# Where the branch for an expert's overflow tokens stands: behind the last expert pass, or in front of it

## Chip, cores and metric

One core of a Trainium2 chip runs the kernel. The metric is the device time of one execution in microseconds (us).

## What is computed

The kernel computes three transformer layers for 256 tokens of width 1024 in float32. The first layer is a block with two kinds of attention and a dense feed-forward. The second and third (here layer 0 and layer 1, as the kernel's code counts them) each have attention, a mixture of 32 experts in four groups, and a gated projection of a per-layer embedding. The expert part and the part behind it, cut from the reference:

```python
def hier_moe(xn, w_group, b_group, w_expert, b_expert, w_gate, w_up, w_down):
    ...
    e_w, e_idx = lax.top_k(e_prob, TOPK_IN_GROUP)          # 2 of the 8 experts of one group
    ...
    cw = jnp.einsum('tk,tke->te', comb, jax.nn.one_hot(expert_id, N_EXPERTS, ...))
    hid = jax.nn.silu(jnp.einsum('td,edf->tef', xt, w_gate)) * jnp.einsum('td,edf->tef', xt, w_up)
    y = jnp.einsum('tef,efd->td', hid * cw[:, :, None], w_down)
    return y.reshape(b, s, d)

# in second_block, for each layer i, behind the attention:
h = h + hier_moe(rms_norm_2(h, ln_ffn[i]), ...)
gate = jax.nn.sigmoid(rms_norm_2(h, ln_ple[i]) @ ple_w_gate[i])
h = h + (gate * (p[i] @ ple_w_proj[i])).astype(h.dtype)
```

## The kernel before

**The expert part** is `moe(l, router, rs)`. It goes over the 32 experts in eight passes `q` of four. Each expert has 32 places for tokens, so a pass has 128 rows. `pick` (in `steps`) builds `T.d`, a 0/1 matrix of tokens by places, on VectorE. A pass then consists of

- `gather` (L993): PE multiplies the activations `hr` with `T.d`, which gives `T.xe`, the tokens in their places;
- `slots` (L1009, L1011): PE transposes `T.d` and fetches the weights of the tokens; ScalarE writes the transposed matrix back into `T.d`;
- `gate_up` (L1025): 64 matmuls of the four experts' gate and up weights against `T.xe`, then `hidden` (L1032 on ScalarE, L1033 and L1034 on VectorE);
- `turn` (L1038 a transpose on PE, L1039 its copy on ScalarE) and `down` (L1045, 16 matmuls; L1049 and L1050 write the result as two parts, `yd`);
- `combine` (L1056): eight matmuls that add `yd` back to the tokens in the four PSUM accumulators `acc`, which also hold the residual.

In the loop, `combine` of pass q - 1 is issued behind `gate_up(q)`, so that PE has work while `hidden(q)` runs on the other engines. For the last combine, L1061 copies the accumulators to `h`.

**Overflow.** If an expert has more than 32 tokens, the rest goes through `Overflow`. `find` picks an expert, `load` fetches its weights (from pass 4 on), and `run` does all of the above for one expert with up to 128 places: `gather` (L993), the transposes L1120 and L1122, 16 matmuls L1129, `turn`, four matmuls L1134, and `combine`. How many such jobs there are is only known on the chip. `over.all` therefore issues the steps in a runtime branch on the count `njob`: `tc.If(n > 0)` around one `run` (L1142), and in it `tc.If(n > 1)` with a loop (L1144, L1145). All five engines take part in the branch, SyncE too. With these inputs layer 0 has one job and layer 1 none.

**Weights** come as a stream: `W.next` hands out pieces of an arena (tiles named `a`), and SyncE issues the loads in the stream's order, each as soon as its piece is free. Behind the experts' weights stand `ple_g` (the gate of the embedding, four loads), then `b_w_q`, the shared key/value weights and `b_w_out` of the next attention. `W.room` and `drop` decide when pieces are free. Tiles of activations (`take`) live in the same arena.

**Behind the experts** comes `ple(l, ...)`: `xt_feats` transposes `h` on PE (L503) and writes it as two parts (`a` at L520 on ScalarE, L521 on VectorE); `proj` multiplies it with `ple_g`, whose tiles are split into two parts (L538, L539), in three matmuls per product (L543 to L545); `gated_part` starts with a tanh at L1226. Eight k steps of six matmuls make one half of the columns; in both layers they are the first thing that runs.

Of the kernel before, what the change touches and what calls it, by code (L numbers as in the profile page):

```python
# [251 lines left out]
def block_kernel(ctx, tc, I, out):  # L252
# [14 lines left out]
    def bank(name="bank"):  # L267
        return psum.tile([128, 512], F32, tag="bank", name=name)

    def sq2(name="sq"):  # L270
        return pr.tile([128, 512], F32, tag="sq", name=name)
# [12 lines left out]
    def drop(*keys):  # L284
        for k in keys:
            arena.drop(k)
        W.pump()
# [120 lines left out]
    def C(name, rows=128):  # L408
        o, n = _COLS[name]
        return cst[:rows, o:o + n]  # L410
# [14 lines left out]
    def drain(g):  # L425
        for _ in g:
            pass
# [22 lines left out]
    def rest(n):  # L450
        for _ in range(n):
            yield

    def chain(*gens):
        for g in gens:
            yield from g
# [26 lines left out]
    class Rstd:  # L483
        def __init__(self, name):
            self.ss = tiny.tile([128, 2, 2], F32, tag="ss", name="ss")
            self.name = name
# [314 lines left out]
    def ple_load(l):  # L801
        pv_ = sq2("ple_p").rearrange("p (t n) -> p t n", t=2)
        nc.sync.dma_start(pv_, I["p_2"][l, 0].rearrange("(t p) n -> p t n", p=128))
        return pv_
# [10 lines left out]
    def ple_proj(pT):  # L815
        pj = take("pj", [2, 1024])
        name, ws = W.next("ple_p")
        for c in range(2):
            ps = [bank("pj") for _ in range(2)]
            for k in range(2):  # L820
                acc_k(pT, k, ws[k][:, c * 512:(c + 1) * 512], ps, k == 0, k == 1)
                yield
            for t in range(2):
                A.copy(pj[:, t, c * 512:(c + 1) * 512], ps[t])
        W.drop(name)
        drop("pT")
        pjs.append(pj)
# [3 lines left out]
    class Step:  # L831


        def __init__(self, d, beside=None):
            self.ahead = ahead = beside is not None
            if ahead:
                self.banks = [bank("ov") for _ in range(3)]
            self.d, self.gub = d, None
            self.sq = beside.sq[:, 256:512] if ahead else sq2("hd")
            self.th, self.hd = self.sq[:, 0:128], self.sq[:, 128:256]  # L840
            self.hT = self.th
            self.ej = tiny.tile([128, 2, 4], F32, tag="ej", name="ej", bufs=4)
            self.cs = tiny.tile([128, 2], F32, tag="cs", name="cs", bufs=4)
            self.xe = self.xet() if ahead else None
            self.yd = [self.ydt() for _ in range(2)] if ahead else []

        def xet(self):
            return sring.tile([128, 8, 128], F32, tag="s", name="xe")
# [14 lines left out]
    def new_d(n):  # L863
        return pr.tile([128, 2, n], F32R, tag="sq", name="d")

    def moe(l, router, rs):
# [114 lines left out]
        def gather(d, Ts, banks=None):  # L981
            Ts = list(Ts)
            n = 128 * len(Ts)
            m = 512 // n
            for T in Ts:
                if not T.ahead:
                    T.xe = T.xet()
            for j in range(8 // m):
                b = bank("g") if banks is None else banks[j % 2]
                for t in range(2):  # L990
                    for i in range(m):
                        for hl in range(2):
                            mm(b[:, i * n:(i + 1) * n], hr[hl][:, t, (m * j + i) * 128:(m * j + i) * 128 + 128], d[:, t],  # L993
                               start=t + i + hl == 0, stop=t + i + hl == m + 1)
                bv = b.rearrange("p (k e s) -> p k e s", k=m, e=len(Ts))
                for e, T in enumerate(Ts):
                    mv = m // 2 if len(Ts) == 1 else m if e == 0 else 0
                    ks = slice(m * j, m * j + mv)
                    if mv:
                        V.tensor_tensor(T.xe[:, ks], bv[:, 0:mv, e],  # L1000
                                        gp[:, ks].unsqueeze(2).to_broadcast([128, mv, 128]), OP.mult)
                    for i in range(mv, m):
                        A.activation(T.xe[:, m * j + i], bv[:, i, e], AF.Copy, scale=gp[:, m * j + i:m * j + i + 1])
                yield

        def slots(q, T):
            b = T.bank("ex")
            for t in range(2):
                nc.tensor.transpose(b[:, t * 128:(t + 1) * 128], T.d[:, t].bitcast(F32), ident)  # L1009
            for t in range(2):  # L1010
                mm(b[:, 256:266], T.d[:, t], cwr[:, t, q], start=t == 0, stop=t == 1)  # L1011
            yield
            A.copy(T.d, b[:, 0:256].rearrange("p (t n) -> p t n", t=2))
            parts = b[:, 256:266].rearrange("p (a e) -> p a e", a=2)
            V.tensor_tensor_reduce(out=T.ej, in0=parts[:, :, 0:4], in1=C("emask").unsqueeze(1).to_broadcast([128, 2, 4]),
                                   scale=1.0, scalar=0.0, op0=OP.mult, op1=OP.add, accum_out=T.cs[:, 0:1])
            V.tensor_reduce(T.cs[:, 1:2], parts[:, :, 4], AX.X, OP.add)
# [34 lines left out]
        def combine(T, last):  # L1052
            for c in range(2):
                for hl in range(2):
                    for t in range(2):
                        mm(acc[t][c], T.d[:, t], T.yd[c][:, hl],  # L1056
                           start=False, stop=last and hl == 1)
                if last:
                    with tc.high_priority():
                        for t in range(2):  # L1060
                            (A.copy if t else V.tensor_copy)(h[:, t, c * 512:(c + 1) * 512], acc[t][c])  # L1061

        class Overflow:
# [75 lines left out]
            def all(self, T, n):  # L1139
                R = Step(new_d(128), T)  # L1140
                self.pick(R.d)
                with tc.If(n > 0):  # L1142
                    self.run(R)
                    with tc.If(n > 1):  # L1144
                        with tc.For_i(1, n, 1):  # L1145
                            self.find()
                            self.load()
                            self.pick(R.d)
                            self.run(R)
                drop("ovg", "ovd", "ovf")  # L1150

        nrs = Rstd(f"rp{l}")
        prev = None
        for q in range(8):
            names, gu, dn = [], [], []
            if q == 6:
                combine(prev, False)
                prev = None
                drain(ple_proj(ple_T(pv_)))
            for i in range(6):  # L1160
                name, v = W.next("gate_up" if i < 4 else "down")
                names.append(name)
                (gu if i < 4 else dn).append(v)
            if q == 2:
                pv_ = ple_load(l)
            if q == 2:
                W.room(4)
            if q == 3:
                over = Overflow()
            if q == 4:  # L1170
                over.load()
                njob_r = nc.values_load(njob_i[0:1, 0:1], min_val=0, max_val=32)
            if q == 5:
                W.room(6 if l else 9)
            if q == 0:
                g = gather(d, Ts)
                next(g)
                acc_h(1, 1)
            T = Ts.pop(0)
            ahead = not Ts and q < 7  # L1180
            if ahead:
                d, Ts = steps()
            if q == 0:
                for i, _ in enumerate(gate_up(0, T, gu)):
                    if i == 1:
                        drain(g)
                        drain(slots(0, T))
                    W.drop(names.pop(0))
            else:
                drain(gate_up(q, T, gu))  # L1190
            if prev is not None:
                combine(prev, False)
            while len(names) > 2:
                W.drop(names.pop(0))
            fill = chain(gather(d, Ts) if ahead else (), slots(q + 1, Ts[0]) if Ts else ())
            for _ in range(0 if q else 3):
                next(fill, None)
            turn(T)
            for _ in range(9 if q else 1):
                next(fill, None)  # L1200
            down(T, dn)
            drain(fill)
            for name in names:
                W.drop(name)
            prev = T
        over.all(T, njob_r)
        drop("hr0", "hr1")
        h = take("h", [2, D])
        combine(T, True)

# [873 lines left out]
```

## Time and profile before

| | before |
|---|---|
| median of 3 runs | 864.68 us (860.13 to 865.07) |
| the profiled execution | 864.54 us |
| its span | 862.8 us |
| PE busy | 823.1 us, 95% of the span |
| DVE, ACT, POOL busy | 61%, 52%, 26% of the span |
| moved by DMA | 201.71 MB, mean 234 GB/s |
| mean granted PE clock | 0.988 of full speed |

[...] The span runs from the first to the last instruction of the trace; what the execution takes beyond it lies outside. Times in rows are microseconds from the span's start. In the page's second part the span is cut into 40 slices of 21.57 us. An "idle before" names what ended it: "DMA" a transfer, an engine's name with "q" its sequencer, "issue" nothing that the profile shows. Consecutive matmuls overlap, so the step from one row to the next is the time of a row, rather than its own duration.

### The profile page before, as it was taken

Reading aid. Unit: us, or ns where it says so; the run is one execution under the profiler, and the core shown is the slowest. Engines: PE = TensorE matmul, PEld = TensorE weight load, DVE = VectorE, ACT = ScalarE, POOL = GpSimd, SP = SyncE. Lnnn points to the kernel's source line nnn. Section 1 sums busy time; section 2 is a strip of 40 time slices with the busy share of each in tenths; the row PEclk is TensorE's granted clock in tenths of the full one; section 3 lists DMA queues with packets and bytes.
Section 4 is the critical chain, followed back from the end, with each engine's and each line's share of the span. In section 5 each row is a group of like instructions: output and inputs, shape, how many; then the busy total and the mean of one; then the engine's idle time right before and its main releaser. Section 6 shows DMA issues by size and latency. Waiting matters only on the chain. (4 is left out here: it accounts for less than half of the span.)

```text
span 862.8 us, 15686 instructions
## 1 busy us (share of the span) xinstructions
PE 823.1 (95%) x5660; PEld 642.2 (74%) x5660; DVE 522.4 (61%) x1520; ACT 447.0 (52%) x1085; POOL 224.3 (26%) x293
## 2 busy tenths in 40 slices
PE   8998999999999999999899999986999999999787
PEld 6896878999999988686667666645878677667456
DVE  5778766755454567678874635423688757353355
ACT  5676865544444456367774133423677743333353
POOL 1224542322222233314553200000224434000011
PEclk9999999999999999999999999999899899999999
DMA  9991529655555542455015699999853426899961
GB/s 320 385 373 43 178 78 398 227 194 167 192 182 194 195 156 99 130 176 208 37 55 198 252 381 404 408 403 377 305 182 124 183 91 258 297 403 406 409 236 49
DMA packets 85714, 201.71 MB, mean 234 GB/s; under 512 B 5840, under 2 KB 27776, under 8 KB 85632
## 3 DMA queue, kind: packets, MB, share of 16 engines
q1 hardware_dynamic: 83568, 198.36, 63.2%
q10 hardware_dynamic: 2064, 2.29, 0.9%
q8 instruction: 47, 0.77, 0.4%
q14 instruction: 35, 0.29, 0.1%
HBM read 199.57 MB, written 1.06 MB: 233 GB/s over the span
## 5 line engine op out<-in xcount | busy, mean ns | idle before, releaser
L539 DVE TENSOR_TENSOR s<-a,s 128x512 fp32r<-128x512 f32 (+3 forms) x281 | 189.9, 686 | 122.7 <-ACT s L538 88.5
L538 ACT CAST s<-a 128x512 fp32r<-128x512 f32 (+3 forms) x294 | 172.5, 601 | 165.6 <-PE pj L545 72.0
L543 PE MATMUL pj<-s,a 128*128 128x512 f32 (+3 forms) x456 | 177.3, 389 | 6.9 <-ACT a L520 5.4
L544 PE MATMUL pj<-s,a 128*128 128x512 f32 (+3 forms) x456 | 171.5, 376 | 3.9 <-DVE s L539 3.8
L539 POOL TENSOR_TENSOR s<-a,s 128x512 fp32r<-128x512 f32 (+3 forms) x71 | 89.3, 1258 | 313.0 <-ACT s L538 280.5
L545 PE MATMUL pj<-s,a 128*128 128x512 f32 (+3 forms) x456 | 170.6, 374 | 0.1
L543 PEld LDWEIGHTS pj<-s,a 128*128 128x128 f32 x456 | 86.8, 190 | 25.6 <-issue 6.2
L544 PEld LDWEIGHTS pj<-s,a 128*128 128x128 f32 x456 | 87.2, 191 | 18.7 <-DVE s L539 6.0
L545 PEld LDWEIGHTS pj<-s,a 128*128 128x128 f32 x456 | 86.9, 191 | 15.9 <-DVE a L521 1.1
L536 POOL TENSOR_SCALAR s<-a 128x512 fp32r<-128x512 f32 (+3 forms) x58 | 40.7, 701 | 221.7 <-PE pj L545 115.2
L1556 PE MATMUL f<-a,s 128*128 128x256 f32 x256 | 72.6, 284 | 0.0
L1558 PE MATMUL f<-a,s 128*128 128x256 f32 x256 | 72.4, 283 | 0.0
L1557 PE MATMUL f<-a,s 128*128 128x256 f32 x256 | 72.4, 283 | 0.0
L1025 PE MATMUL gu<-a,xe 128*32 128x256 f32 x1024 | 61.0, 380 | 5.0 <-DMA a<-in_moe_w_up_dram 4.3
L1025 PEld LDWEIGHTS gu<-a,xe 128*32 128x32 f32 x1024 | 33.6, 110 | 33.8 <-issue 11.5
L543 PE MATMUL acc<-s,a 128*128 128x512 f32 x128 | 50.1, 391 | 0.0
L544 PE MATMUL acc<-s,a 128*128 128x512 f32 x128 | 49.9, 390 | 0.0
L545 PE MATMUL acc<-s,a 128*128 128x512 f32 x128 | 49.8, 389 | 0.0
L1557 PEld LDWEIGHTS f<-a,s 128*128 128x128 f32 x256 | 49.1, 192 | 0.2
L1556 PEld LDWEIGHTS f<-a,s 128*128 128x128 f32 x256 | 49.1, 192 | 0.2
L1558 PEld LDWEIGHTS f<-a,s 128*128 128x128 f32 x256 | 49.1, 192 | 0.0
L640 POOL TENSOR_SCALAR P<-P,nd 128x128 f32<-128x128 f32 x64 | 30.5, 489 | 51.5 <-DVE nd L635 22.1
(359 smaller groups left out, 1413.3 us busy)
## 6 DMA issues: line engine op xcount, KB each, us to landing
a<-in_moe_w_gate_dram SPq DMA_DIRECT2D x66, 512.0 KB, 7.1
a<-in_moe_w_up_dram SPq DMA_DIRECT2D x66, 512.0 KB, 8.3
a<-in_w_ff_dram SPq DMA_DIRECT2D x32, 1024.0 KB, 5.6
a<-in_moe_w_down_dram SPq DMA_DIRECT2D x32, 1024.0 KB, 10.2
a<-in_a_w_in_dram SPq DMA_DIRECT2D x10, 1024.0 KB, 5.1
a<-in_ple_w_gate_dram SPq DMA_DIRECT2D x8, 1024.0 KB, 15.6
a<-in_w_in_dram SPq DMA_DIRECT2D x6, 1024.0 KB, 14.0
a<-in_w_o_dram SPq DMA_DIRECT2D x4, 1024.0 KB, 13.3
```

The source lines that it names most:

```text
L536: G.tensor_scalar(hi, wv, 1.0, 0.0, OP.mult, OP.add)
L538: A.copy(hi, wv)
L539: (G if nsplit[0] % 5 == 2 else V).tensor_tensor(lo, wv, hi.bitcast(F32), OP.subtract)
L543: mm(ps, xh, hi, start=st, stop=False)
L544: mm(ps, xh, lo, start=False, stop=False)
L545: mm(ps, xl, hi, start=False, stop=sp)
L640: G.tensor_scalar(p[:, o0:o0 + n], p[:, o0:o0 + n], rc[:, t, i:i + 1], 1.0, OP.mult, OP.mult)
L1025: mm(b[32 * e:32 * e + 32, 0:256], T.xe[:, k, 32 * e:32 * e + 32], w, start=k == 0, stop=k == 7)
L1556: mm(o, hi[:, fs], xt[0][:, k], start=st, stop=False)
L1557: mm(o, hi[:, fs], xt[1][:, k], start=False, stop=False)
L1558: mm(o, lo[:, fs], xt[0][:, k], start=False, stop=sp)
```

## The change

`over.all` is called in the loop at the end of pass 6 instead of behind the loop, in both layers. Three things go with it. `combine(6)`, which was issued behind `gate_up(7)`, is issued in `all`, ahead of the branch; `prev = None` keeps it from being issued again. The tiles `R.yd` of the overflow step are allocated there instead of in `Step`. And at q == 6 the filler work (`slots(7)`) goes behind `down(6)` instead of around it. The activations `hr0`, `hr1` are dropped after pass 6. Line numbers of the changed kernel are those of before plus 2 from L1142 on (the branch is L1144, its inner ones L1146 and L1147) and plus 9 behind the loop.

```diff
@@ Step.__init__
-            self.yd = [self.ydt() for _ in range(2)] if ahead else []
+            self.yd = []
@@ Overflow.all
                 self.pick(R.d)
+                combine(T, False)
+                R.yd = [R.ydt() for _ in range(2)]
                 with tc.If(n > 0):
@@ the loop over q
             fill = chain(gather(d, Ts) if ahead else (), slots(q + 1, Ts[0]) if Ts else ())
+            later = rest(0)
+            if q == 6:
+                fill, later = later, fill
             for _ in range(0 if q else 3):
                 next(fill, None)
             turn(T)
@@
             down(T, dn)
             drain(fill)
+            drain(later)
             for name in names:
                 W.drop(name)
             prev = T
-        over.all(T, njob_r)
-        drop("hr0", "hr1")
+            if q == 6:
+
+                over.all(T, njob_r)
+                drop("hr0", "hr1")
+                prev = None
         h = take("h", [2, D])
         combine(T, True)
```

PE in layer 0, the way into the branch. In the kernel before, from the combine of pass 6, which stands behind the 32 last matmuls of gate_up(7) (`y_6295`, `y_6303` are the results of down(7)):

```order
L1056 MATMUL acc<-yd,d 128x512 x8
L1038 MATMUL ht<-ident_r,hd 128x128
L1045 MATMUL y_6295<-a_6100,hd 32x512 x2
L1045 MATMUL y_6295<-a_6163,hd 32x512 x2
L1045 MATMUL y_6303<-a_6100,hd 32x512 x2
L1045 MATMUL y_6303<-a_6163,hd 32x512 x2
L1142 COMPARE_AND_BRANCH
L993 MATMUL ov<-d,a_5050 128x128
```

In the changed kernel, from the turn of pass 6 (`y_6212`, `y_6220` are the results of down(6)):

```order
L1038 MATMUL ht<-ident_r,hd 128x128
L1045 MATMUL y_6212<-a_5880,hd 32x512 x2
L1045 MATMUL y_6212<-a_5882,hd 32x512 x2
L1045 MATMUL y_6220<-a_5880,hd 32x512 x2
L1045 MATMUL y_6220<-a_5882,hd 32x512 x2
L1009 MATMUL ex<-ident_r,d 128x128 x2
L1011 MATMUL ex<-cwr,d 128x10 x2
L1056 MATMUL acc<-yd,d 128x512 x8
L1144 COMPARE_AND_BRANCH
L993 MATMUL ov<-d,a_5050 128x128
```

The branch has come forward past gate_up(7), the turn and down(7); combine(6) now stands directly in front of it, and slots(7) has moved behind down(6).

PE in layer 0, the way out of the branch, from the last matmuls of the loop's body (which is not entered) on. Before:

```order
L1056 MATMUL acc<-yd,d 128x512 x8
L1145 REGISTER_ALU
L1145 COMPARE_AND_BRANCH
L1145 UNCONDITIONAL_BRANCH
L1144 UNCONDITIONAL_BRANCH
L1142 UNCONDITIONAL_BRANCH
L1056 MATMUL acc<-yd,d 128x512 x8
L503 MATMUL tps<-ident_r,a_6524 128x128 x8
```

In the changed kernel, first the way out, and then (behind the gate_up(7) that begins there) from the turn of pass 7 on:

```order
L1056 MATMUL acc<-yd,d 128x512 x8
L1147 REGISTER_ALU
L1147 COMPARE_AND_BRANCH
L1147 UNCONDITIONAL_BRANCH
L1146 UNCONDITIONAL_BRANCH
L1144 UNCONDITIONAL_BRANCH
L1025 MATMUL gu<-a_5884,xe 32x256
```

```order
L1038 MATMUL ht<-ident_r,hd 128x128
L1045 MATMUL y_6504<-a_6100,hd 32x512 x2
L1045 MATMUL y_6504<-a_6163,hd 32x512 x2
L1045 MATMUL y_6512<-a_6100,hd 32x512 x2
L1045 MATMUL y_6512<-a_6163,hd 32x512 x2
L1056 MATMUL acc<-yd,d 128x512 x8
L503 MATMUL tps<-ident_r,a_6524 128x128 x8
```

Behind the branch now stands gate_up(7) with no combine between it and its turn, and the last combine follows down(7) with no branch between.

SyncE in layer 0, the loads in front of the branch, from the last of `ple_g` on. Before:

```order
L299 DMA a_6207<-in_ple_w_gate_dram 128x4x512
L299 DMA a_6236<-in_b_w_q_dram 128x4x512
L299 DMA a_6238<-in_b_w_q_dram 128x4x512
L299 DMA a_6284<-in_b_w_q_dram 128x4x512
L299 DMA a_6286<-in_b_w_q_dram 128x4x512
L299 DMA a_6288<-in_w_kv_shared_dram 128x8x256
L299 DMA a_6290<-in_w_kv_shared_dram 128x8x256
L299 DMA a_6311<-in_b_w_out_dram 128x4x512
L299 DMA a_6313<-in_b_w_out_dram 128x4x512
L1142 COMPARE_AND_BRANCH
```

In the changed kernel:

```order
L299 DMA a_6205<-in_ple_w_gate_dram 128x4x512
L299 DMA a_6207<-in_ple_w_gate_dram 128x4x512
L299 DMA a_6236<-in_b_w_q_dram 128x4x512
L299 DMA a_6238<-in_b_w_q_dram 128x4x512
L1144 COMPARE_AND_BRANCH
```

Six loads (two of `b_w_q`, the two shared ones and two of `b_w_out`) have moved from in front of the branch to behind it.

## Rows read from the trace of the kernel before

**Rows 1.** the page: busy time of the engines; granted clock and memory traffic in 40 slices

```profile
PE 823.1 (95%) x5660; PEld 642.2 (74%) x5660; DVE 522.4 (61%) x1520; ACT 447.0 (52%) x1085; POOL 224.3 (26%) x293
...
PEclk9999999999999999999999999999899899999999
...
GB/s 320 385 373 43 178 78 398 227 194 167 192 182 194 195 156 99 130 176 208 37 55 198 252 381 404 408 403 377 305 182 124 183 91 258 297 403 406 409 236 49
```

**Rows 2.** timeline of PE, layer 0 (start, us, engine, line, operation, count, [idle before, releaser])

```profile
568.14 0.30 PE L1038 MATMUL ht<-ident_r,hd 128*128 128x128 f32 x1 [1.37 <-DVE hd L1034]
568.28 0.38 PE L1009 MATMUL ex<-ident_r,d 128*128 128x128 f32 x2
...
568.80 1.92 PE L1045 MATMUL y<-a,hd 128*32 128x512 f32 x16
570.54 1.07 PE L1025 MATMUL gu<-a,xe 128*32 128x256 f32 x6
573.57 3.61 PE L1025 MATMUL gu<-a,xe 128*32 128x256 f32 x58 [1.96 <-DMA a<-in_moe_w_up_dram]
577.11 2.13 PE L1056 MATMUL acc<-yd,d 128*128 128x512 f32 x8
579.08 0.27 PE L1038 MATMUL ht<-ident_r,hd 128*128 128x128 f32 x1
579.71 1.92 PE L1045 MATMUL y<-a,hd 128*32 128x512 f32 x16 [0.35 <-ACT hd L1039]
581.56 3.79 PE L993 MATMUL ov<-d,a 128*128 128x128 f32 x32
...
595.80 2.11 PE L1056 MATMUL acc<-yd,d 128*128 128x512 f32 x8 [0.42 <-PEq L1144]
598.93 1.09 PE L503 MATMUL tps<-ident_r,a 128*128 128x128 f32 x8 [1.02 <-DVE a L1061]
603.65 0.80 PE L543 MATMUL pj<-s,a 128*128 128x512 f32 x1 [3.63 <-ACT a L520]
```

**Rows 3.** timeline of ACT, layer 0, the first feature write

```profile
603.13 0.47 ACT L520 ACTIVATE a<-tps,small 128x256 fp32r<-128x256 f32 x1 [3.02 <-SPq L1144]
```

**Rows 4.** timeline of SP, layer 0, the weight loads behind ple_g

```profile
577.85 10.23 SPq L299 DMA_DIRECT2D a<-in_b_w_q_dram  x4
...
596.82 8.26 SPq L299 DMA_DIRECT2D a<-in_b_w_out_dram  x4
```

**Rows 5.** timeline of PE, layer 1, passes 6 and 7 and what follows

```profile
813.77 1.92 PE L1045 MATMUL y<-a,hd 128*32 128x512 f32 x16
...
819.04 3.61 PE L1025 MATMUL gu<-a,xe 128*32 128x256 f32 x58 [1.96 <-DMA a<-in_moe_w_up_dram]
...
825.18 1.92 PE L1045 MATMUL y<-a,hd 128*32 128x512 f32 x16 [0.35 <-ACT hd L1039]
827.28 1.64 PE L1056 MATMUL acc<-yd,d 128*128 128x512 f32 x6 [0.18 <-PEq L1142]
831.41 1.01 PE L1056 MATMUL acc<-yd,d 128*128 128x512 f32 x2 [2.49 <-issue]
832.22 1.91 PE L503 MATMUL tps<-ident_r,a 128*128 128x128 f32 x8
833.84 0.80 PE L543 MATMUL pj<-s,a 128*128 128x512 f32 x1
```

**Rows 6.** DMA of the stretch 828.5 to 831 (queue, packets, MB, share)

```profile
q8 instruction: 1, 0.02, 2.8%
```

**Rows 7.** busy time by stretch; behind the engines: granted clock, DMA share, GB/s

```profile
560.00:580.00 20.00, 16.30 (x177) 9.65 (x179) 4.21 (x14) 4.99 (x11) 0.00 (x0) 1.00 1.03 405
...
602.40:609.20 6.80, 5.55 (x15) 4.48 (x16) 3.77 (x13) 5.13 (x14) 0.00 (x0) 0.50 1.07 373
...
831.10:834.50 3.40, 3.09 (x12) 2.58 (x12) 2.11 (x4) 1.39 (x3) 0.00 (x0) 0.50 0.51 187
```

**Rows 8.** line 1226, its waits for the projection, first in each layer (first, last start)

```profile
L1226 ACTq EVENT_SEMAPHORE  x2: 17/17/17, 617.0 to 844.3; - x2
```

## The prediction, made before the changed kernel was run

> **What bounds the kernel now.** The page comes first: TensorE is busy for 95% of the span and its granted clock is below full in only a few of the 40 slices [rows 1], so time is won where TensorE stands still or runs at half clock. Then the timeline of TensorE around the overflow branch, in both expert layers. In layer 0 one job exists and the body runs; three spots of that row list matter [rows 2]. Pass 7's gate/up matmuls stop for 1.96 us for the last up weight and go on at 573.57. Pass 7's own turn, down and combine follow, the body runs from 581.56, and the last combine starts at 595.80. And the first gate projection of the next stage (L543) starts only at 603.65, after 3.63 us of idle. What ends last there is ScalarE: its first L520, the write of the transposed features, sat 3.02 us for "SPq L1144" [rows 3]. It writes into the arena piece that held the overflow weights, so it needs SyncE to have passed the branch, and SyncE has queued six more weight loads in front of that branch: its issues run from 577.85 to 605.1 [rows 4], over 2 us each, while memory moves 377 to 408 GB/s [rows 1]. In layer 1 no job exists and the branch is jumped [rows 5]: the last combine begins at 827.28, stops after six of eight matmuls, and the last two start at 831.41 after 2.49 us of "issue", that is a wait for nothing that the profile shows. In the 2.5 us around that hole there is one transfer of the queue "q8 instruction", 0.02 MB [rows 6]; that PE jumped to a place whose following instructions had not been fetched is my reading of the two rows. After both holes the granted clock is 0.50: for 6.8 us in layer 0, for 3.4 us in layer 1 [rows 7].
>
> **The change part by part, layer 0.** The body (with its drain and exit) stands in front of pass 7. From the end of down(6), 568.80 + 1.92 = 570.7 [rows 2], PE now does:
> - slots(7), which used to lie in the wait for hT and now stands behind down(6): 568.80 - 568.28 = 0.52, to 571.2. It costs 0.5, since the hT wait that hid it stays.
> - combine(6), 579.08 - 577.11 = 1.97, to 573.2. It now fills the time in which the up weight lands, so the 1.96 us wait goes.
> - the body and its exit, 595.80 - 581.56 = 14.24, to 587.4. Its weights were loaded from pass 4 on, in front of both places.
> - gate_up(7), all 64 matmuls behind the branch: 58 take 577.11 - 573.57 = 3.54, so 64 take 3.9, to 591.3. Six of them used to be done before the wait.
> - the hidden step without cover. Before, combine(6) lay there; now PE waits 1.37 as it does in front of the turn of pass 6 [rows 2], to 592.7. Then turn to down 579.71 - 579.08 = 0.63 and down 581.56 - 579.71 = 1.85, to 595.2; and 0.18 for the eviction as in layer 1 [rows 5].
> So the last combine starts at 595.35 instead of 595.80: this half of the change is nearly nothing (-0.45), what the weights' wait gives is paid back to the bare hidden step. From the last combine to L503 it is 598.93 - 595.80 = 3.13 in either kernel, so L503 at 598.5. Now SyncE: it has only four ple_g and two b_w_q issues in front of the branch; at 10.23 / 4 = 2.56 us each from 577.85 on [rows 4] the second is out at 583, before the body ends, and the arena hands the features another piece, that of pass 7's last expert, which gate_up(7) reads last. The 3.02 us wait goes. ScalarE's L520 then starts 603.13 - 3.02 - 598.93 = 1.18 after L503, at 599.7, and L543 another 603.65 - 603.13 = 0.52 later, at 600.2. That is -3.45 us. What is late next is the chain of transposes and L520 itself, which PE waits for about 1.1 us.
>
> The clock is the second half. The eight k steps from L543 to the first L1226, which reads the finished first column half, take 617.0 - 603.65 = 13.35 in layer 0 [rows 2, 8], with its stretch at 0.50, and 844.3 - 833.84 = 10.46 in layer 1 [rows 5, 8], where only the first 0.66 us are at half clock. The fall follows the 3.63 us idle. With an idle near 1.1 I take full clock: -2.9. Bounds: 0, if the clock falls all the same, and -2.9. I take the far end because TensorE stood 1.96 us in 560 to 580 at a clock of 1.00 [rows 2, 7]. Layer 0: -6.3.
>
> The six loads moved behind the branch are not free: SyncE issues them from 587.4 on, and most need pieces that gate_up(7) frees at 591.3, instead of 583 to 605. They are 6 MB, at about 390 GB/s (between the 377 and 408 of [rows 1]) 15 us, so they land by about 606; that is no later than the last b_w_out issue before, which ended at 605.1 [rows 4] and had still to land. No wait for them is on PE's row before 603.65, so I cost them at nothing; if the queue drains into a hole they could be 3 us late, and that is in the range.
>
> **Layer 1.** Here only combine(6), the jump and pass 7 follow one another. down(6) ends at 813.77 + 1.92 = 815.7, slots 0.5, combine(6) 1.97: PE is at gate_up(7) by 818.2, and the last up weight is there at 819.04 as before (the transfers are bound by memory, not by PE). 819.04 + 3.9 + 1.3 + 0.63 + 1.85 + 0.2 puts the last combine at 826.9 instead of 827.28; its eight matmuls have no branch between, so L503 comes 3.13 later at 830.1, against 832.22, and L543 at 831.8 against 833.84: -2.0. The first 0.66 us of the projection ran at half clock there (to 834.5 [rows 7]), 0.3 more. Unknown is what the jump costs at its new place: nothing, if the target is fetched by then, up to the 2.49 us of before, counted from the end of combine(6): 818.2 + 2.49 = 820.7, which is 1.6 later than the weights. I take nothing, since 0.8 us of the wait for the weights would hide a third of it and the branch of before cost 0.18 [rows 5] where its target was there. Layer 1: -2.3, with +1.6 on it as the other end.
>
> The sum against the profiled execution: 864.54 - 6.3 - 2.3 = 855.9, where 1.7 us lie outside the span in both kernels. The median of the runs is 864.68, 0.1 above it, so 856. ScalarE's order at the start of the gate projection also shifts, so that the second weight split (L538) comes behind one more pair of feature writes; I allow 0 to 1.3 us for that and take 0.
>
> [...]
>
> **The rivals.**
> 1. *The fetch moves with the branch.* PE waits 2.49 us behind the branch in front of pass 7, in layer 1 for the jump (1.6 past the weights) and in layer 0 for the way out of the body (2.49 - 0.42 = 2.1 more than before). Then 855.9 + 1.6 + 2.1 = 859.6. For it: the hole exists [rows 5]. Against it: layer 0 leaves its body by the same jump before with 0.42 us of PE idle [rows 2].
> 2. *The wait of ScalarE goes, the clock does not come back.* 864.54 - 3.45 - 2.0 = 859.1. For it: the stretch between the last combine and L543 still has PE idle for most of 3 us with 1.1 us of matmul in it.
> 3. *Slower: the branch starves the clock ahead of pass 7.* PE's idles of 2.49 and 3.63 us were followed by 0.50, those of 1.96 were not. If PE stands over 2.5 us at the branch in front of gate_up(7), pass 7 (3.9 + 0.63 + 1.85 + 1.97 = 8.35 us of PE time) takes that much again. In both layers, with the projection of layer 0 still slow and 1.6 us of fetch in layer 1: 2 x 8.35 + 1.6 - 3.45 - 2.0 = +12.9: 877.4. In layer 1 alone: 8.35 + 1.6 - 6.3 - 2.0 = +1.7: 866.2. Against it: in layer 0 the body is PE work to its end.
> 4. *It does not do what it says.* SyncE still reaches the branch late because the first two b_w_q issues wait for pieces: then ScalarE's wait stays and layer 1 alone gains, 864.54 - 2.3 = 862.2. Against it: they are issued from 577.85 on, without a wait for the branch [rows 4].
>
> **How the numbers follow.** The forecast has 58% (its own range 853 to 858), rival 2 18%, rival 1 11%, rival 3 7%, rival 4 6%. The range from 852.5 to 863.5 holds all of them but the slow case; its lower end allows 3.5 us more than the sum, for the terms that I took in full against the change (0.5 for slots(7), 1.37 for the bare hidden step) and for a projection at less memory pressure. One per cent, about what a measurement of this kernel can tell from no change, is 8.6 us, so the forecast lies on that edge. Faster by over 1%: 0.40, some two thirds of the forecast's share. Slower by over 1%: 0.04, rival 3 in both layers (in layer 1 alone it stays within). Within 1%: 0.56.
>
> **What would show it.** Right: in layer 0 no wait of ScalarE's L520 for SyncE, L543 at 600 to 601, granted clock 1.00 from 600 to 610, the first L1226 near 611; SyncE's b_w_q list split in two with a gap; in layer 1 the eight matmuls of the last combine in one piece, gate_up(7) at 819 to 820, L543 near 832. Wrong: an idle of PE above 2 us in front of the first gate_up(7) matmul (rival 1, with the clock below it rival 3), a stretch of 0.50 after L503 (rival 2), or L520 still waiting for SyncE (rival 4). If all steps hold and the time is still above 860, the gain has been given back in layer 1's attention, where VectorE's splits and not PE end last.

## The result, and the profile after

The changed kernel takes 858.99 us in the median of 20 runs (853.97 to 863.07), the kernel before 863.33 us in 20 runs on the same chips; the ratio is 0.9949 (0.9933 to 0.9965). That is 4.4 us faster, half of the 8.6 us forecast, though the profiled execution took 855.65 us, where 855.9 was worked out. The runs lie in groups: nine from 853.97 to 855.76, eleven from 858.56 to 863.07. The profiled one is of the first group, and the median is not; where the second comes from is the main question of the experiments. One slow run of the experiments, 1342.61 us at a mean granted clock of 0.557, is left out of every number below.

The page of the changed kernel, its engines, clock and memory traffic, against [rows 1]:

```profile
PE 817.7 (96%) x5660; PEld 639.4 (75%) x5660; DVE 522.8 (61%) x1520; ACT 445.1 (52%) x1085; POOL 226.5 (27%) x293
...
PEclk9999999999999999999999999999999999999999
...
GB/s 319 385 376 54 155 74 399 238 178 192 198 197 178 171 152 151 64 244 124 125 1 188 264 333 406 406 409 385 370 221 127 195 106 247 304 405 406 409 245 50
```

PE is busy for 5.4 us less with as many instructions: what went is time at half clock (the mean granted clock of the execution is 0.994 instead of 0.988). The timeline of PE in layer 0, from down(6) to the first projection matmul, answers to [rows 2]:

```profile
569.20 1.92 PE L1045 MATMUL y<-a,hd 128*32 128x512 f32 x16 [0.36 <-ACT hd L1039]
571.06 0.44 PE L1009 MATMUL ex<-ident_r,d 128*128 128x128 f32 x2
...
571.47 2.09 PE L1056 MATMUL acc<-yd,d 128*128 128x512 f32 x8
573.40 3.69 PE L993 MATMUL ov<-d,a 128*128 128x128 f32 x32
...
587.76 3.99 PE L1025 MATMUL gu<-a,xe 128*32 128x256 f32 x64 [0.65 <-PEq L1146]
593.01 0.30 PE L1038 MATMUL ht<-ident_r,hd 128*128 128x128 f32 x1 [1.26 <-DVE hd L1034]
593.67 1.92 PE L1045 MATMUL y<-a,hd 128*32 128x512 f32 x16 [0.35 <-ACT hd L1039]
595.52 2.35 PE L1056 MATMUL acc<-yd,d 128*128 128x512 f32 x8
597.71 1.06 PE L503 MATMUL tps<-ident_r,a 128*128 128x128 f32 x8
599.62 0.50 PE L543 MATMUL pj<-s,a 128*128 128x512 f32 x1 [0.85 <-ACT a L520]
```

The wait for the up weight is gone, gate_up(7) runs in one piece behind the body, and L543 starts 0.85 us after PE falls idle instead of 3.63. ScalarE's first feature write and SyncE's loads in layer 0, against [rows 3, 4]:

```profile
599.10 0.84 ACT L520 ACTIVATE a<-tps,small 128x256 fp32r<-128x256 f32 x2
```

```profile
579.01 11.35 SPq L299 DMA_DIRECT2D a<-in_b_w_q_dram  x4
591.83 7.03 SPq L299 DMA_DIRECT2D a<-in_w_kv_shared_dram  x2
```

L520 waits for nothing that is late. SyncE itself reaches the branch of layer 0 at 583.9 instead of 602.1 (the branch instruction on SyncE's queue, first start of two, in the kernel before and in the changed one):

```profile
L1142 SPq COMPARE_BRANCH  x2: 44/44/45, 602.1 to 823.4; - x2
```

```profile
L1144 SPq COMPARE_BRANCH  x2: 44/44/45, 583.9 to 813.9; - x2
```

Layer 1, against [rows 5]:

```profile
800.01 3.66 PE L1025 MATMUL gu<-a,xe 128*32 128x256 f32 x64
...
805.75 2.61 PE L1045 MATMUL y<-a,hd 128*32 128x512 f32 x16 [0.36 <-ACT hd L1039]
...
812.13 3.99 PE L1025 MATMUL gu<-a,xe 128*32 128x256 f32 x64 [0.41 <-DMA a<-in_moe_w_down_dram]
...
819.89 2.36 PE L1056 MATMUL acc<-yd,d 128*128 128x512 f32 x8
822.09 1.07 PE L503 MATMUL tps<-ident_r,a 128*128 128x128 f32 x8
823.99 0.50 PE L543 MATMUL pj<-s,a 128*128 128x512 f32 x1 [0.83 <-ACT a L520]
...
829.17 0.50 PE L544 MATMUL pj<-s,a 128*128 128x512 f32 x1 [0.97 <-DVE s L539]
```

The last combine is whole. New is the last row: in the projection PE waits 0.97 us for a weight split. The clock in two stretches, against [rows 7] (the last two columns are DMA share and GB/s):

```profile
599.60:611.60 12.00, 11.98 (x54) 9.29 (x55) 11.30 (x29) 8.81 (x21) 4.90 (x3) 1.00 1.07 368
...
806.90:810.30 3.40, 3.40 (x15) 1.81 (x8) 1.54 (x5) 1.54 (x3) 0.00 (x0) 0.51 1.02 404
```

Layer 0's projection is at full clock. A new stretch of half clock lies in layer 1 over down(6) and combine(6).

For all that follows, the profiled executions are cut at the same five marks: the start of gate_up(6) and of the first L543 in each layer, and the first tanh of layer 0. Each number is a difference of start times in the traces, in us. The mark of the tanh is its own instruction (ACTIVATE), and not the semaphore row of the same line that [rows 8] show: that row stands 0.67 us ahead of the tanh in layer 0 of the kernel before, 1.96 us ahead of it in layer 1 (844.34 and 846.30), and the changed kernel has none in layer 0. The first tanh of the kernel before and of the changed one (first start; line 1226 has become 1235):

```profile
L1226 ACT ACTIVATE th<-pj,rph x9: 475/682/692, 617.7 to 858.2; 128x512 f32<-128x512 f32 x7, 128x256 f32<-128x256 f32 x2
```

```profile
L1235 ACT ACTIVATE th<-pj,rph x4: 671/678/691, 611.6 to 628.0; 128x512 f32<-128x512 f32 x4
```

| profiled execution | layer 0: gate_up(6) to L543 | to the first tanh | on to gate_up(6) of layer 1 | layer 1: gate_up(6) to L543 | on to the end |
|---|---|---|---|---|---|
| before | 40.54 | 14.05 | 190.47 | 25.67 | 28.92 |
| changed | 36.24 | 11.98 | 188.41 | 23.98 | 29.88 |
| changed, again | 36.24 | 11.97 | 189.45 | 30.20 | 29.90 |
| layer 0 only | 36.23 | 11.99 | 188.38 | 25.37 | 29.15 |
| layer 1 only | 41.53 | 13.12 | 190.43 | 24.10 | 29.88 |
| fewer loads in front | 39.78 | 11.54 | 190.45 | 25.78 | 28.90 |
| changed, shift 40 | 36.23 | 11.97 | 188.40 | 24.00 | 29.90 |
| changed, shift 216 | 36.46 | 11.98 | 189.49 | 24.10 | 29.90 |
| before, shift 126 | 41.29 | 13.10 | 190.41 | 23.21 | 29.21 |
| slots(7) in the wait | 35.96 | 11.98 | 188.36 | 23.54 | 29.92 |
| slots(7) in the wait, again | 36.01 | 11.98 | 188.44 | 23.38 | 29.94 |
| slots(7) in the wait, shift 40 | 35.99 | 11.98 | 188.46 | 22.66 | 29.92 |
| the same, again | 35.97 | 11.98 | 190.54 | 22.53 | 29.92 |
| layer 0 only, slots(7) in the wait, shift 126 | 38.33 | 11.98 | 189.54 | 23.08 | 29.22 |

### The profile page after: what moved, and what is told of

Read it like the earlier page. It is cut to its first block, busy times and chain, and to the rows that moved or that the text cites. A ratio compares the mean times of both kernels' runs of the same rounds, so it can differ in the third digit from the quotient of the medians.

```text
span 853.9 us, 15690 instructions
## 1 busy us (share of the span) xinstructions
PE 817.7 (96%) x5660; PEld 639.4 (75%) x5660; DVE 522.8 (61%) x1520; ACT 445.1 (52%) x1085; POOL 226.5 (27%) x293
## 5 line engine op out<-in xcount | busy, mean ns | idle before, releaser
L539 DVE TENSOR_TENSOR s<-a,s 128x512 fp32r<-128x512 f32 (+3 forms) x281 | 189.6, 685 | 118.2 <-ACT s L538 85.7
L543 PE MATMUL pj<-s,a 128*128 128x512 f32 (+3 forms) x456 | 176.0, 386 | 5.4 <-ACT a L520 3.9
L539 POOL TENSOR_TENSOR s<-a,s 128x512 fp32r<-128x512 f32 (+3 forms) x71 | 91.2, 1284 | 329.6 <-ACT s L538 287.7
L543 PEld LDWEIGHTS pj<-s,a 128*128 128x128 f32 x456 | 86.1, 189 | 23.8 <-issue 5.9
L543 PE MATMUL acc<-s,a 128*128 128x512 f32 x128 | 50.1, 391 | 0.0
```

The lines of the kernel that those rows point to most:

```text
L539: (G if nsplit[0] % 5 == 2 else V).tensor_tensor(lo, wv, hi.bitcast(F32), OP.subtract)
L543: mm(ps, xh, hi, start=st, stop=False)
```

## The experiments

**The changed kernel again.** No edit.

> The changed kernel once more, unedited. Its 20 runs lie in three groups, 854 to 856, 858.5 to 860.5 and 861 to 863 us, the profiled one in the first. Theory A: the groups differ by stretches of half clock that fall or do not fall at some place of PE work outside the two layers' branches (a good guess is layer 1's attention, where the profile of before has one at 670.7); then this profile has the same times as the first around both branches (L543 at 599 to 601 in layer 0), and if it is of a slower group, its extra half clock and its extra time lie between 620 and 800. Rival B: the groups come from the branch itself (a fetch or a wait that is sometimes there); then a slower profile has its extra time between 570 and 600 or between 808 and 824. Median 857 to 860 by both.

Median of 12 runs 860.01, ratio 0.9952 (0.9924 to 0.9981); five runs from 854.92 to 855.49, seven from 858.96 to 863.22. This time the profiled execution, 862.62 us, is of the second group. Its layer 1:

```profile
810.39 2.10 PE L1056 MATMUL acc<-yd,d 128*128 128x512 f32 x8
817.91 5.17 PE L1025 MATMUL gu<-a,xe 128*32 128x256 f32 x64 [5.41 <-PEq L1144]
```

PE stands for 5.41 us at the branch, and then runs a part of gate_up(7) at half clock (0.50 from 817.2 to 820.6). The branch instruction on PE (both layers: shortest, median and longest in ns, first and last start), of the first profile and of this one:

```profile
L1144 PEldq COMPARE_BRANCH  x2: 86/980/1875, 572.6 to 809.8; - x2
```

```profile
L1144 PEldq COMPARE_BRANCH  x2: 86/3200/6314, 572.3 to 811.2; - x2
```

Layer 0, which falls through into the body, has the 86 ns; layer 1, which jumps, 1.88 us and 6.31 us. The page of the kernel before has this for the queue of [rows 6]:

```profile
q8 instruction: 47, 0.77, 0.4%
```

That is 0.016 MB in each transfer, beside 5660 matmuls and 5660 weight loads of PE, so by estimate one for about 241 of them; from 100 to 500 us 20 transfers stand beside 5096, one for 255. One such transfer is what the expectations below call a block. That the queue serves PE is inferred: in [rows 5, 6] and in the second profile here PE stands still until one of its transfers has run. In the first profile one begins ahead of the jump, in 808.5 to 809.8:

```profile
q8 instruction: 1, 0.02, 5.3%
```

In the second one that queue moves nothing from 802 to 814.5; its transfer begins in 814.5 to 815.5, over 3 us behind the jump:

```profile
q8 instruction: 1, 0.02, 7.7%
```

So rival B was right for this execution, and theory A explains 1.0 us of it at most (189.45 - 188.41, with a clock of 0.51 in layer 1's attention from 670.4 to 673.8): in the first profile the transfer is on its way when PE jumps, in the second it is not. That costs 30.20 - 23.98 = 6.2 us, about the distance from the first group to the runs above 860.

It is not shown for all the slower runs. Of the 32 runs of the changed kernel 14 lie from 853.97 to 855.76, six from 858.56 to 859.77, all at a mean granted clock of 0.991, and twelve from 860.28 to 863.22 at 0.989 to 0.993; only one of the twelve is profiled. Nine of the first 14 have 0.996, with a median of 855.2. From 0.996 to 0.991 is 0.5% of 857 us, about 4.3 us at most, and 855.2 + 4.3 = 859.5: by this estimate the six can be half clock alone, without the long branch. The six of the twelve that have 0.993 can't be, since by the same estimate they would take about 857.8 us.

**The change in one layer alone.** `cond` is `l == 0` or `l == 1`; the other layer calls `over.all` behind the loop as before (the swap of the fillers, `combine` in `all` and the place of `R.yd` follow the same condition).

```diff
-            if q == 6:
+            if q == 6 and cond:
                 over.all(T, njob_r)
                 ...
+        if not cond:
+            over.all(T, njob_r)
+            drop("hr0", "hr1")
```

> The branch in front of the last pass in layer 0 alone, layer 1 as before. Theory A: layer 0 carries the larger part, about 6 of the 9 us between the two profiles: L543 of layer 0 at 599 to 601, no half clock there, the hole of 2.49 us in the last combine of layer 1 is back; profile 857 to 859 us, median 860 to 861. Rival B (the clock's share is chance, only ScalarE's wait is real): L543 at 600 but the time from L543 to the first L1226 as long as before, 13 us; profile 860 to 861.

> The branch in front of the last pass in layer 1 alone, layer 0 as before. Theory A: layer 0 has its wait of 3 us for SyncE and the half clock behind it again, layer 1 gains 2 to 3 us: last combine in one piece, L543 of layer 1 some 27 us behind the start of gate_up(6) instead of 25.7 plus 2; profile 861 to 863 us. Rival B: with layer 0 undone the phase of the clock in layer 1 changes and the gain there goes; profile 864 to 865.

Layer 0 alone: 855.71 us, 9 runs, eight of them from 854.41 to 856.28; ratio 0.9923 (0.9899 to 0.9948), better than the whole change. Layer 1 alone: 867.23 us, 12 runs, none under 861.3; ratio 1.0059 (1.0029 to 1.0088), slower than before. The first went as theory A had it, with more gain than its 860 to 861. The second did not: 861 to 863 was expected, and the profile (863.99) is one of the better executions, with a branch of 1.07 us. Layer 1's share is a loss in the medians, though its part of this one profile is 0.6 us shorter than before (24.10 + 29.88 against 25.67 + 28.92). Layer 0 alone keeps the old hole in layer 1, whose PE rows read as in [rows 5]:

```profile
817.13 1.41 PE L1056 MATMUL acc<-yd,d 128*128 128x512 f32 x5 [0.18 <-PEq L1145]
821.28 1.11 PE L1056 MATMUL acc<-yd,d 128*128 128x512 f32 x3 [2.74 <-issue]
```

It now comes after five matmuls, not six, which fits a place in PE's program and not an operation; the shift of 126 instructions below tests it.

**Fewer loads in front of the branch.** The kernel before, with the stream held back for pass 7 of layer 0.

```diff
+            if q == 7 and l == 0:
+                W.room(15)
...
         over.all(T, njob_r)
+        if l == 0:
+            W.room(9)
```

> The kernel before with one thing taken from the change: in layer 0 the six weight loads that stood in front of SyncE's branch are issued behind it (the stream's limit is lowered for pass 7 and set back behind the branch); the branch itself stays behind the last pass, and layer 1 is untouched. Theory A: SyncE reaches the branch before the body ends, ScalarE's 3.02 us wait for it shrinks to under 0.5, L543 comes at 600 to 601 instead of 603.65 and the half clock behind it goes, so the eight k steps take 10.5 to 11 us: 5 to 6.5 us faster, 858 to 860, the same gain as the change brings in layer 0. Rival C (the place of the body in front of pass 7 itself is worth something): gain under 3 us.

858.67 us, 12 runs, ratio 0.9951 (0.9931 to 0.9971): faster by 4.7. Layer 0 behind the body:

```profile
601.18 1.09 PE L503 MATMUL tps<-ident_r,a 128*128 128x128 f32 x8 [0.99 <-DVE a L1061]
602.79 0.50 PE L543 MATMUL pj<-s,a 128*128 128x512 f32 x1 [0.51 <-ACT a L520]
```

From L503 to L543 it is 1.61 instead of 4.72 us (-3.1), and the steps to the first tanh take 11.54 instead of 14.05 (-2.5). With the branch where it was (SyncE reaches it at 583.5), moving the six loads alone brings 5.6 us there, near the 3.0 and 2.9 that I had worked out for SyncE's wait and the clock behind it. This execution gives 2.4 of them back in gate_up(7), whose matmuls behind the wait for the up weight are slower:

```profile
574.13 5.30 PE L1025 MATMUL gu<-a,xe 128*32 128x256 f32 x58 [1.96 <-DMA a<-in_moe_w_up_dram]
```

That is no accident of one run: of the four profiles with layer 0's old order, three (this one, layer 1 alone, and before with shift 126) take 5.30 us for these 58 matmuls, the kernel before 3.61. The 1.69 more is what 3.4 us at half clock cost, so I take it for half clock; that is an estimate from the two durations. With the branch in front of pass 7 that wait is gone. So the place of the body is worth something too, as rival C had it: from gate_up(6) to the first tanh layer 0 alone takes 36.23 + 11.99 = 48.2 us, fewer loads 39.78 + 11.54 = 51.3, and the medians differ by as much (855.71 and 858.67), though the intervals of the two ratios overlap.

**PE's program shifted.** If the fetch of the jump's target is the cause, adding instructions far ahead of the branch should change it, since that moves every place in PE's program. Where a block ends is an estimate here, from the 241 to 255 matmuls and loads of a block and the start of one transfer; no run shows it to the instruction. The changed kernel with 20 more matmuls in the warm-up:

```diff
-    warm(12, bank("warm"))
+    wb = bank("warm")
+    warm(8, wb)
+    for _ in range(24):
+        mm(wb[:, 0:32], ones_b, ones_b[:, 0:32], start=True, stop=True)
```

> The changed kernel with PE's program shifted by 40 instructions (20 more matmuls of 32 columns in the warm-up at the very start, four of the 512-column ones fewer). Theory D: the runs of 861 to 863 us are those in which layer 1's jump in front of pass 7 comes before the block of instructions with its target has been asked for; the shift has that block asked for some 40 instructions earlier, while gate_up(6) still runs. Then PE's COMPARE_BRANCH of layer 1 takes under 1 us instead of 1.9 or 6.3, gate_up(7) follows without a wait for it, and all runs lie in 853 to 857, median 855 (-1%). Rival E: the slow group comes from half-clock stretches that only chance sets, the branch's 6.3 us being their consequence; then the shift changes nothing, median 858 to 860 with both groups.

856.56 us, 6 runs from 855.25 to 856.95, no second group; ratio 0.9929 (0.9901 to 0.9956). The branch:

```profile
L1147 PEldq COMPARE_BRANCH  x2: 86/258/430, 573.9 to 811.5; - x2
```

0.43 us. Theory D holds, at a cost of 1.3 us: layer 0's gate_up(6) starts at 564.65 instead of 563.38, and with the shorter warm-up the second and third matmul of the first projection take 0.69 and 0.59 us in this execution, where the changed kernel has 0.44 for each.

> The same with a shift of 216 instructions (2 full and 118 small matmuls in the warm-up, about 2 us more there), which puts layer 1's branch shortly in front of a block's end, so that its target lies two blocks on. Theory D: the jump always waits for the fetch, COMPARE_BRANCH of layer 1 takes 6 to 6.5 us in every execution, there is no fast group, all runs in 860 to 866. Rival E: two groups as before, each about 2 us later.

The place follows by estimate: in the first profile the transfer begins by 809.3 and the branch comes at 809.8, with slots(7) and combine(6), 24 matmuls and loads, in front of it, so the branch stands up to 24 behind a block's start, and with the shift up to 240, near the 241 to 255 of a block. The body is 65 matmuls and as many loads and stands twice between the branch and its target, 260, about one block more. That such a target always has to be waited for was an assumption; no run shows it.

862.70 us; of nine runs two are at 856 and 858 and seven from 862.3 to 866.6; ratio 1.0002 (0.9973 to 1.0032). Theory D's "in every execution" missed: the profiled execution, one of the two, has a branch of 1.41 us. The shift made the slower runs the rule, which is the direction that D gave; that those seven have the long branch is not seen, as none of them is profiled.

> The kernel before, with PE's program shifted by 126 instructions (2 full and 73 small matmuls in the warm-up), so that the target of layer 1's jump lies early in a block instead of shortly in front of a block's end. Theory D: the hole of 2.49 us in the last combine of layer 1 goes and with it the half clock behind it (831.1 to 834.5), layer 0 stays as it was: 2.5 to 3.5 us faster, median 860. Rival E: the hole stays or moves to another matmul of the combine, no change.

In the kernel before PE stops six matmuls and their loads, 12 instructions, behind the target, and a transfer begins at 829.1, inside the hole; so by estimate a block ends there, and the shift puts the target 126 - 12 = 114 behind that end.

862.55 us, 12 runs, ratio 1.0000 (0.9979 to 1.0022). The hole went, as the last combine shows:

```profile
827.91 2.10 PE L1059 MATMUL acc<-yd,d 128*128 128x512 f32 x8 [0.18 <-PEq L1145]
```

Layer 1 gains 25.67 - 23.21 = 2.5 us, but the time does not follow: this execution starts gate_up(6) of layer 0 1.5 later, and takes 5.30 us for the 58 matmuls of its gate_up(7). On the hole theory D held: a shift of PE's program alone removed it; on the time it missed.

**slots(7) back in the wait.** The changed kernel without its swap.

```diff
-            if q == 6:
-                fill, later = later, fill
```

> The changed kernel without its swap of the fillers at q == 6: slots(7) stands in front of down(6) again, in the wait for the transposed hidden tile, in both layers. My sum charged 0.5 us per layer for the swap. If that is right, the turn-to-combine stretch of pass 6 gets 0.5 shorter in both layers, in layer 1 hidden by the wait for the weights. It also moves where PE's program crosses into the next block relative to its waits by 8 instructions, so the share of runs with the long branch may change either way; profile 854 to 855.5 or 860 to 862, by the branch.

> The changed kernel with slots(7) in the wait once more, unshifted. Its five runs so far had no slow group, with a COMPARE_BRANCH of 2.16 us in layer 1 and the fetch only 0.3 us ahead of it. Theory D: the block is asked for so late here that the slow group must show with more runs, a third to a half of them at 859 to 861. Rival F: standing slots(7) in front of down(6) is enough, since PE then has 8 instructions fewer between the block's edge and the branch; no run above 858.

853.40 us in 5 runs, ratio 0.9909 (0.9877 to 0.9940), and the second time 854.26 in 8 runs, ratio 0.9920 (0.9888 to 0.9951). One run of the 13 lies above 858, at 859.71. Rival F fits better than D, though the branch takes 2.16 and 2.02 us in the two profiles (when the transfer begins in them, no row here shows); the one run has a mean granted clock of 0.990 where the three lowest beside it have 0.999, so half clock alone can make it. With the shift on top (11 full and 21 small matmuls):

> The changed kernel with slots(7) in the wait again and with PE's program shifted by 40 instructions (11 full and 21 small matmuls in the warm-up). Theory D: both hold together; COMPARE_BRANCH of layer 1 under 1 us, no group above 858, gate_up(7) of layer 1 about 11 to 11.6 us behind gate_up(6), median 852.5 to 854.5 (-1.0 to -1.2%). Rival E (groups by chance): runs above 859 come back among these.

> The same shifted by 40 instructions, once more beside it. Theory D: no run above 858, median 852.5 to 855.5.

855.00 us in 6 runs and 854.16 us in 6, each with a ratio of 0.9896 (0.9867 to 0.9925, and 0.9864 to 0.9928), no run above 856.8. This is the version with the lowest ratio, faster than before by 1.04%, with layer 1 in 22.66 + 29.92 = 52.6 us; its interval overlaps with that of the unshifted one, so the 40 instructions show no gain in time here. The first median is half a microsecond above what was expected.

**The old order of layer 1 with its hole closed.** Layer 0 alone changed, slots(7) in the wait, shift 126 (9 full and 66 small matmuls).

> The branch in front of the last pass in layer 0 alone, with slots(7) in the wait there, layer 1 as before, and PE's program shifted by 126 instructions (9 full and 66 small matmuls in the warm-up), so that layer 1's jump has no hole behind it. If layer 1's share of the change is worth less than closing the hole of the old order, as the times of layer 1 from gate_up(6) to the end say (52.4 against 53.9), this is the fastest: layer 1 in 52 to 53 us, profile 850 to 853, median 851 to 853.5. If the old order's advantage there was chance of the clock, it is as fast as the changed kernel with slots(7) in the wait or slower, 853.5 to 855.

857.46 us, 6 runs, ratio 0.9928 (0.9902 to 0.9953): missed. Layer 1 took 52.3 us as expected; but the shift opened a hole in layer 0, behind the body's way out:

```profile
587.18 2.78 PE L1028 MATMUL gu<-a,xe 128*32 128x256 f32 x43 [0.54 <-PEq L1150]
592.03 1.49 PE L1028 MATMUL gu<-a,xe 128*32 128x256 f32 x21 [2.08 <-issue]
```

So 126 instructions that take the hole out of layer 1 (2.49 us in the kernel before) bring one of 2.08 into layer 0.

## Why the prediction was right or wrong

The sum met the profiled execution within 0.3 us, by errors that cancel, and by luck: the profiled execution was one of the shorter group, and the median lies 3 us above the forecast.

- *SyncE's wait, -3.45.* Right in kind; 40.54 - 36.24 = 4.3 was measured. The 0.85 more lies behind the last combine, where I carried over 3.13 us to L503: it takes 597.71 - 595.52 = 2.19, since VectorE no longer has splits in front of its L1061 copies (before, three L539 in 1.90 us from 596.38 and the copies from 598.19; now the copies from 596.94 and L539 behind them). Moving only the loads shows the wait by itself (3.1, from L503 to L543).
- *The clock behind it, -2.9.* The stretch at 0.50 went, but the steps to the first tanh became only 2.1 shorter (14.05 to 11.98). Two things were wrong. I read 13.35 and 10.46 off the semaphore rows of line 1226 [rows 8], which do not stand at the same distance from the tanh; to the tanh itself the two layers took 14.05 and 846.30 - 833.84 = 12.46, so the difference that I took for the clock was 1.6 in these rows and not 2.9. And with the old order on ScalarE and no half clock (the first L543 takes 0.50 us in fewer loads, 0.80 in the kernel before) the steps take 11.54: the clock is worth 2.5, and the 0.44 up to 11.98 is the term for ScalarE's order, "0 to 1.3", which I took at 0. In layer 1 the same order costs 29.88 - 28.92 = 1.0, with PE's wait of 0.97 for a split in its row. This is the first step that failed: a priced term was set to nothing without a row that hid it, beside a term read off the wrong row.
- *The place of the body, "nearly nothing".* So it is against the profile of before (the last combine starts 32.14 behind gate_up(6) instead of 32.68), but that execution was the one of four in which pass 7's matmuls behind the wait for the up weight took 3.61 us and not 5.30; against the other three the change saves 2.3 to 2.6 us more. The prediction had taken 1.96 us of idle as safe from the rows of that one execution.
- *slots(7) behind down(6), 0.5.* Back in the wait it saves 0.28 in layer 0 (36.24 to 35.96) and 0.44 in layer 1.
- *The loads behind the branch, 0.* No wait for them appears; SyncE sends the shared weights from 591.8 on.

*Layer 1, -2.3, "I take nothing" for the jump, 1.6 as its other end.* This is the step that cost the median. In the good case the jump costs 1.9 us, and PE then waits 0.41 for a weight; L543 comes 1.7 earlier, ScalarE's order takes 1.0 back, and 0.7 is left. In the bad case it costs 6.3 us and half clock behind it, and the layer loses 54.59 to 60.10, that is 5.5 us. My upper end came from the 2.49 us hole, which is only the uncovered rest of a fetch: in the kernel before PE's branch was reached at 825.2 and the hole ended at 831.4, 6.2 us later, with down(7) and six matmuls of the combine running meanwhile. Its start is there in the row of the branch in the kernel before, which I did not read (second of the two; its own 342 ns are not the price):

```profile
L1142 PEldq COMPARE_BRANCH  x2: 86/214/342, 579.8 to 825.2; - x2
```

Rival 1 is what happens in layer 1 in the second profile of the changed kernel, with the long branch of 6.31 us, whose instruction transfer begins over 3 us behind the jump; its price was too small, and in layer 0 it does not happen (0.65 us of idle in front of gate_up(7)).

*What I did not have at all:* 2.1 us between the layers (190.47 to 188.41). In the profile of before, 6.8 us of layer 1's attention ran at 0.50, in that of the changed kernel none:

```profile
670.70:677.50 6.80, 6.08 (x28) 4.32 (x28) 4.56 (x23) 4.69 (x19) 0.35 (x1) 0.50 0.37 119
```

The stretch can come with the change too: the version with slots(7) in the wait and shift 40 has it in its second profile, as long, while its first, at a mean granted clock of 0.999, had none:

```profile
663.50:670.30 6.80, 6.31 (x30) 4.32 (x28) 4.56 (x23) 4.68 (x17) 0.12 (x1) 0.50 0.34 108
```

But it is not plain chance either. The third column of the table is 190.4 to 190.5 in all four profiles in which layer 0's branch stands behind the last pass, and in one of the ten in which it stands in front; three of the ten have 189.5 (one of them is the changed kernel again, with its 3.4 us at 0.51), and six 188.4 to 188.5 (the changed kernel's clock is 1.00 from 662 to 678; in layer 0 alone the 16 matmuls of line 624 that take 2.93 us in the stretch of the kernel before take 1.58). So the change in layer 0 seems to make the stretch rarer; by what, no run shows.

Of the 8.9 us between the two profiles 6.4 belong to layer 0, 0.7 to layer 1 and 2.1 to this stretch, less 0.3 that the changed one lost ahead of gate_up(6). The medians add up: layer 0 alone brings 7.6, between its 6.4 and the 8.4 with the stretch; layer 1 alone costs 3.9, and 3.7 together is near the 4.4 of the change. Rival 2 and rival 4 did not happen. Rival 3 happened in a small way: half clock does fall on pass 7 behind the long branch, for 3.4 us (0.50 from 817.2 to 820.6) and not for the whole pass.

Open is what decides in the changed kernel whether the instructions at the target have been asked for in time; only one profile of the second group exists. That the runs above 860 have the long branch is inferred from their absence with the shift of 40 (none of 18 runs above 857), not seen, and the runs from 858.5 to 860 may be half clock alone. Nor is it settled why the median of layer 1 alone is 3.9 us longer when its one profile shows no such loss, nor why the attention's half clock comes in some executions alone.

## What to carry to other kernels

A wait that ends on another engine's queue can be removed by what stands in that queue: six loads in front of a branch held up a whole stage, and moving them alone took that wait and the half clock behind it away (5.6 us of its profile), though not all that moving the branch in layer 0 brought. A runtime jump can have the price of a fetch of instructions: 6.2 us here, of which down(7) and six matmuls covered 3.7 in the kernel before; with 40 instructions more at the program's start the branch took 0.43. Put it behind long work that is already queued, and read the branch instruction itself, its duration and its start, not only the hole that is left. Before two times are subtracted, see that both rows are the same kind of instruction. When one profile and the median disagree, profile the same kernel again before explaining either.

## What the runs showed of the hardware that I had not expected

One and the same branch of one kernel took 1.88 us in one execution and 6.31 in the next, and 40 instructions more at the program's start brought it to 0.43. The granted clock fell to 0.50 behind idles shorter than the 1.96 us after which it had stayed at 1.00: in layer 1 of the changed kernel at 806.9, behind 1.43 and 0.36 us, where 1.50 and 0.36 us in front of the same rows of layer 0 had left it at 1.00 (560 to 580). And 1.96 us is not safe: in three other profiles (layer 1 alone, fewer loads, before with shift 126) pass 7's wait for the up weight in layer 0, 1.95 to 1.97 us behind a shorter one of 0.44 to 0.76, was followed by 58 matmuls in 5.30 us instead of 3.61, by the estimate above 3.4 us at half clock. In these runs the length of the last idle by itself does not decide it, as rival 3 had assumed.
